# TensorE's order from modelled queues of VectorE, ScalarE, GpSimd and of PSUM's banks

## The chip, the cores and the metric

The kernel runs on one core of a Trainium2 chip. What counts is the device time of one execution in microseconds (us), as the median of several runs; smaller is better.

## The reference

One layer of a hybrid backbone for 256 context tokens and 2048 latent tokens of width 1024. One input projection feeds three token mixers; each is gated, and one output projection closes the layer.

```python
h = rmsnorm(x, g_pre) * (1 + scale) + shift
u_m, u_rs, u_rz, u_l = split(h @ w_in)
y_m = mlstm_branch(u_m)        # 6 heads of 64, chunkwise, one pass in each direction
y_r = rwkv_branch(u_rs, u_rz)  # 6 heads of 64, state S = S*w - (S kh) b + v kt, in each direction
y_l = rglru_branch(u_l)        # 256 channels: convolution, then a scan in each direction
o = concatenate([y_m, y_r, y_l]) @ w_out
return x + gate * rmsnorm(o, g_post), new states
```

Context tokens start from empty states and latent tokens from the cached ones; a direction's latent scan starts where its context scan ended.

## The kernel before

Everything is held with features or tokens on 128 partitions, and a projection of full precision is split into high and low parts, so that one block of 512 tokens costs three matmuls for each of eight slices of the contraction (`hhi`, `hlo` against `whi`, `wlo`, `w`). The stages, in the order of time:

- **build_h** normalises a block of tokens (`x`), transposes it (`tp`) and writes `hhi` and `hlo`. A block here is 256 context tokens or 512 latent tokens; blocks 1 and 0 come first, then 2, 3 and 4, each normed as its turn begins.
- **the projector** makes the columns of the input projection (`pp_v`, `pp_mk`, `pp_rz`, ...). Its matmuls depend on nothing late, so they are the filler of all stages up to the chains.
- **shift_post** makes the shifted RWKV inputs, and writes transposed values (`vs`) through SP's queue to the chunk store `ch`.
- **derive** runs 54 blocks of the RWKV preparation. For a block TensorE computes `pw`, ScalarE and VectorE make `KB` of it (the last step on line 972), and TensorE multiplies parts of it (`pt`). A round of 32 chunks (the trace has seven rounds) then goes to GpSimd, which solves a triangular system `W` in 30 pairs of instructions (lines 1058 and 1060), and comes back through a transposed `XT` into `pY` and `pX`.
- **mlstm** computes the chunks of the matrix memory: `pd` for its states, `pm` and `pn` for its outputs; GpSimd norms the result `H` (line 1344), and TensorE transposes it (`hT`).
- **chains**: three chains (two heads each) walk through 36 chunks forward and then 36 backward. A step loads `cg` from `ch`, makes a small product `cq`, ScalarE copies it into `q` (line 1630), a second product goes back into `cg` (VectorE, line 1644, in the first direction; ScalarE, line 1642, in the second), a third gives the next state (VectorE, line 1659). `ga` and `gb` prepare two steps at a time. The scans of the RG-LRU and the gates run beside the first direction, and the output projection of the mLSTM part (`po`) fills it.
- **out_last**: where all twelve parts of 128 tokens are in `yr`, they are normed, transposed (`yT`), gated into `zhi` and `zlo`, and multiplied by `w_out` (`pz`).

Tile, the framework, orders the instructions of all engines but TensorE. TensorE's order is planned by the class `Flow`, while the program is written out: each stage is a generator, and `run` always continues the ready one of the best rank (chains 1, workers such as derive and mlstm 2, out_last 3, filler 9). `F.now` is a clock that counts only the modelled time of the matmuls issued so far. Where a generator needs another engine's result, it yields a constant number of nanoseconds: what it assumes that the result takes. `LAT` (11000) stands between `pw` and `pt`, 40500 before `XT`, 7000 and 3000 around `pY`, 9000 before `hT`, `WAIT` or, until the scans are over, `LONG` between the parts of a chain's step, 4200 and 3800 (`L1`, `L2`) before `yT` and `pz`. No constant knows what else stands in an engine's queue, and a full PSUM does not move the clock.

## Time and profile before

| what | us |
| --- | --- |
| median of 3 runs (2066.2 to 2070.28) | 2069.45 |
| the profiled execution, its own time | 2059.59 |
| its span | 2057.9 |
| TensorE busy | 1801.6 |
| VectorE, ScalarE, GpSimd busy | 1367.0, 977.6, 795.0 |
| TensorE's mean granted clock | 0.933 |

The execution is cut into eight stretches where the work changes: at 103 us the start-up is over; at 577 the last `pp_v` ends, at 638 derive's first `pw` runs, at 1042 its last `pX`; at 1378 the chains' first `ga` runs, at 1726 they turn round, at 2018 the last `cq` is over. In each stretch the length less TensorE's busy time is its idle time; the eight idle times add up to 256.4 us. A wait row says which engine waited at which line for which result, and how long in total, how often, and at most. The last row's kind, the chain that ended last, gives the time per matmul when matmuls follow one another: a row of six 512-wide ones or of sixteen small ones.

### The profile page before, as it was taken

What the parts mean: (1) busy time and instruction counts of PE and PEld (TensorE: products, weight loads), DVE (VectorE), ACT (ScalarE), POOL (GpSimd) and SP (SyncE); (2) the same over time, 40 slices, a digit from 0 to 9 for tenths busy, and PEclk for the clock granted to TensorE, in tenths of its full rate; (3) what the DMA queues carried; (4) which work ended last, traced back from release to release, by engine and by line L of the source; (5) the groups of instructions that cost most, each with busy time, mean ns of one, the idle gap of its engine ahead of it and who ended that gap; (6) DMA issues with size and microseconds to landing.
All of it is one profiled execution on the core that took longest, in us unless ns stands there. A gap on an engine that the chain in (4) does not pass through costs nothing. (4 is left out here: it accounts for less than half of the span.)

```text
span 2057.9 us, 46221 instructions
## 1 busy us (share of the span) xinstructions
PE 1801.6 (88%) x16648; PEld 1201.0 (58%) x16778; DVE 1367.0 (66%) x3271; ACT 977.6 (48%) x2634; POOL 795.0 (39%) x1200
## 2 busy tenths in 40 slices
PE   5899999999999878788899798878778788999996
PEld 3555655656666556555566565555555556777774
DVE  3747366777643898998324766647885576777774
ACT  5732446565434667776242545542332233444442
POOL 0210011112110688888722444342653232444442
PEclk9899999999999988889999899989888999999997
DMA  7343344564548778887254666645986545576662
GB/s 284 118 142 90 126 123 133 153 168 148 132 127 247 215 207 223 225 214 176 80 154 135 188 171 170 171 118 154 292 268 193 164 136 149 163 196 203 197 190 72
DMA packets 353370, 350.60 MB, mean 170 GB/s; under 512 B 109554, under 2 KB 294978, under 8 KB 350728
## 3 DMA queue, kind: packets, MB, share of 16 engines
q1 hardware_dynamic: 353142, 347.65, 59.2%
q8 instruction: 133, 2.18, 0.5%
q14 instruction: 95, 0.78, 0.1%
HBM read 211.18 MB, written 136.37 MB: 169 GB/s over the span
## 5 line engine op out<-in xcount | busy, mean ns | idle before, releaser
L1635 POOL TENSOR_SCALAR sd<-cg,Dall 128x128 f32<-128x128 f32 x210 | 135.8, 654 | 267.1 <-DVE cg L1659 164.0
L1659 DVE SCALAR_TENSOR_TENSOR cg<-cq,Dall,sd 64x64 f32<-64x64 f32 x408 | 114.5, 281 | 46.4 <-PE cq L168 36.6
L1060 POOL TENSOR_TENSOR W<-W,tmp 128x30 f32<-128x30 f32 (+14 forms) x210 | 139.0, 662 | 16.1
L1058 POOL TENSOR_TENSOR tmp<-W 128x30 f32<-128x30 f32 (+14 forms) x210 | 133.0, 633 | 15.9
L168 PE MATMUL cq<-cg,bt 128*64 128x64 f32 x840 | 68.5, 246 | 49.7 <-DVE cg L1644 44.6
L1283 ACT ACTIVATE nb<-nb,aT 128x128 f32<-128x128 f32 x216 | 71.6, 393 | 82.5 <-DMA nb<-nm_d 72.4
L168 PE MATMUL cq<-cg 128*64 128x64 f32 x1728 | 92.9, 230 | 8.2 <-DVE cg L1659 8.2
L168 PEld LDWEIGHTS cq<-cg,bt 128*64 128x64 f32 x840 | 44.1, 142 | 84.9 <-DVE cg L1644 54.8
L168 PE MATMUL ga<-cg 64*64 64x128 f32 (+1 forms) x864 | 76.9, 270 | 16.9 <-DMA cg<-ch 16.9
L1630 ACT ACTIVATE q<-cq 128x64 f32<-128x64 f32 x216 | 45.5, 223 | 95.7 <-PE cq L168 92.3
L1592 DVE TENSOR_TENSOR cg<-gb,rmask 64x256 f32<-64x256 f32 x108 | 44.7, 413 | 66.3 <-PE gb L168 61.1
L168 PEld LDWEIGHTS cq<-cg 128*64 128x64 f32 x1728 | 72.9, 141 | 24.3 <-issue 9.5
L168 PE MATMUL pz<-owhi,zhi 128*128 128x512 f32 x180 | 82.1, 456 | 4.5 <-ACT zhi L1822 4.5
L1598 ACT ACTIVATE bt<-ga 128x256 f32<-128x256 f32 x108 | 41.3, 383 | 87.0 <-DVE G L1595 83.4
L168 PE MATMUL pt<-KB 64*64 64x64 f32 x864 | 41.9, 244 | 45.7 <-DVE KB L972 45.6
L1284 POOL TENSOR_SCALAR_AFFINE_SELECT nb<-nb 128x256 f32<-128x256 f32 x108 | 44.8, 421 | 93.0 <-ACT nb L1283 63.6
L168 PE MATMUL gb<-cg 64*64 64x128 f32 (+1 forms) x864 | 75.7, 270 | 0.9 <-DMA cg<-ch 0.9
L168 PE MATMUL pz<-owhi,zlo 128*128 128x512 f32 x180 | 73.5, 409 | 3.3 <-DVE zlo L1823 3.3
L168 PE MATMUL pz<-owlo,zhi 128*128 128x512 f32 x180 | 72.9, 405 | 0.0
L168 PEld LDWEIGHTS ga<-cg 64*64 64x64 f32 x864 | 48.2, 142 | 41.9 <-issue 27.9
L168 PE MATMUL cq<-q,cg 128*64 128x64 f32 x864 | 59.4, 236 | 9.9 <-ACT q L1630 9.9
L168 PE MATMUL pp_v<-hhi,whi_v 128*128 128x512 f32 (+1 forms) x120 | 67.4, 562 | 0.3 <-ACT whi_v L514 0.3
(511 smaller groups left out, 6180.0 us busy)
## 6 DMA issues: line engine op xcount, KB each, us to landing
cg<-ch SPq DMA_DIRECT2D x216, 192.0 KB
wa<-wa SPq DMA_DIRECT2D x54, 256.0 KB
z<-z SPq DMA_DIRECT2D x27, 512.0 KB
ch<-KB SPq DMA_DIRECT2D x108, 128.0 KB
ch<-KB SPq DMA_DIRECT2D x54, 256.0 KB
nb<-nm_d SPq DMA_DIRECT2D x108, 128.0 KB
lr<-L SPq DMA_DIRECT2D x16, 768.0 KB
lL<-lr SPq DMA_DIRECT2D x16, 768.0 KB
```

The source lines that it names most:

```text
L168: self.nc.tensor.matmul(out, lhsT, rhs, start=start, stop=stop, **kw)
L1058: nc.gpsimd.tensor_tensor(out=tv, in0=W[:, j + 1:32, j:j + 1].to_broadcast([128, m, j]), in1=W[:, j:j + 1, 0:j].to_broadcast([128, m, j]), ...
L1060: nc.gpsimd.tensor_tensor(out=W[:, j + 1:32, 0:j], in0=W[:, j + 1:32, 0:j], in1=tv, op=ALU.add)
L1283: nc.scalar.activation(nb[:, d, j], nb[:, d, j], AF.Exp, bias=aT[:, c, d, 2 * p + j:2 * p + j + 1])
L1284: nc.gpsimd.affine_select(out=nb[:, d], in_=nb[:, d], pattern=[[0, 2], [1 - 2 * d, 128]], base=0, channel_multiplier=-1 + 2 * d, compare_o ...
L1592: nc.vector.tensor_tensor(out=cg[o, :, RK[h]], in0=src[o], in1=mask[o, d].rearrange("p a c -> p (a c)")[:, None].to_broadcast([64, 2, 128] ...
L1598: nc.scalar.activation(bt, ga[:, 1], AF.Copy)
L1630: nc.scalar.activation(q, qk, AF.Copy, scale=-1.0)
L1635: nc.gpsimd.tensor_scalar(sd, cg.rearrange("p (n c) -> p n c", c=64)[:, 0::9], Dk, None, op0=ALU.mult)
L1659: nc.vector.scalar_tensor_tensor(out=nxt[h][b], in0=ps[b], scalar=Dk[b], in1=sd[b, 1 - h], op0=ALU.mult, op1=ALU.add)
```

## The change

Every VectorE, ScalarE and GpSimd instruction now passes through a proxy that writes down when it would start and end: a modelled cost, a queue for each engine, behind its inputs. PSUM's eight buffers are followed in the same way. `when(tile)` tells how far a tile's modelled end lies ahead of `F.now`, and takes the place of nearly all constants; `least` keeps a lower bound. `stand`, called before each matmul, moves `F.now` to the time at which the matmul's inputs and its bank are there. `First` marks instructions that Tile gives priority, so that the model lets them overtake.

Apart from that, `norm(b + 1)` is issued in the middle of block b (`norm(2)` right after the first two blocks) and `fetch` one block earlier; `H` is split in two tiles and `yr` in eighteen. The gates' and the scans' own constants and the loading of `w_out` stay. Instructions are the same: 11,330 matmuls, 1448 DMAs, and as many VectorE, ScalarE and GpSimd operations; only their order and their waits differ.

```diff
+class Queue:
+        def call(*a, **k):
+            r = f(*a, **k)
...
+            self.F.issued(self.kind, name, out, [x for x in aps if x is not out], k.get("accum_out"))
+            return r
...
+class Banks:
+    def tile(self, *a, **k):
+        t = self.pool.tile(*a, **k)
+        self.names.append(t.tensor.name)
+        if len(self.names) > self.n:
+            self.F.before[t.tensor.name] = self.names[-1 - self.n]
+        return t
...
+    TO, BETWEEN, FROM = 260.0, 90.0, 130.0
+    def cost(self, kind, op, n):
+        if kind == "a":
+            return 190.0 + 0.78 * n
+        if kind == "g":
+            return 150.0 + 1.05 * n if op in ("memset", "affine_select") else 330.0 + 2.0 * n
...
+        return 155.0 + (0.65 if op in ("tensor_copy", "tensor_scalar", "memset") else 0.97) * n
+    def issued(self, kind, op, out, ins, extra):
...
+        if kind == "v" and all(x.space != PSUM for x in [out] + ins) and any(a < t + d and t < b for a, b in self.taken["g"]):
+            d *= 1.35
+        if self.first:
+            for a, b in q:
+                if a <= t < b:
+                    t = b
+                    break
+        else:
+            for a, b in q:
+                if t + d <= a:
+                    break
+                t = max(t, b)
...
+    def when(self, *tiles, least=0.0):
+        return max([least] + [self.wrote.get(x.tensor.name, 0.0) + self.FROM - self.now for x in tiles])
+    def stand(self, out, *ins):
+        b = self.before.pop(out.tensor.name, None)
+        t = max([self.wrote.get(x.tensor.name, 0.0) + self.FROM for x in ins] + [self.read.get(b, 0.0) + self.FROM])
+        self.now = max(self.now, t)
...
     def mm(self, out, lhsT, rhs, start=True, stop=True, **kw):
+        self.stand(out, lhsT, rhs)
...
+            elif k + 1 == NK:
+                fetch(3)
...
+        norm(2)
         for b in range(2, len(BLOCKS)):
-            norm(b)
-            if b + 1 < len(BLOCKS):
-                fetch(b + 1)
+            if b + 2 < len(BLOCKS):
+                fetch(b + 2)
+            yield F.when(*xs[b])
             for k in range(NK):
+                if k == 4 and b + 1 < len(BLOCKS):
+                    norm(b + 1)
...
-                yield 1500.0
+                yield F.when(vr, *nxt) if d else F.when(vr)
...
             sid, l0, nm, KB = block()
-            yield LAT
+            yield F.when(KB, least=3000.0)
...
-        yield 40500.0
+        yield F.when(W)
...
-        yield 9000.0
+        yield F.when(HH[g])
...
-            wait = LONG if X["lru"].t is None else WAIT
+            wait = WAIT
...
-            yield wait[0], 1
+            yield F.when(q, least=wait[0]), 1
...
-            yield wait[1], 1
+            yield F.when(cg, least=wait[1]), 1
...
-        yield L1, 1
+        yield max(0.0, F.last + F.FROM - F.now), 1
...
-        yield L2
+        yield F.when(*[x for p in parts for x in p[1:]])
```

What that does to TensorE's order is shown at three places; a name's numbers tell the block or step, and a row ends with the shape and the count. The first is derive's first round, before; `pt` and `pw` come in runs, with filler after the run:

```order
L168 MATMUL pt_0_2560_6048<-KB_0_2560_5827 64x64 x8
L168 MATMUL pw_0_5121_6065<-wa_0_5121_5751,w_2_01_5729 128x256 x4
L168 MATMUL pt_0_2561_6094<-KB_0_2561_5865 64x64 x8
L168 MATMUL pw_0_7680_6109<-wa_0_7680_5883,w_2_00_5689 128x256 x4
L168 MATMUL pt_0_5120_6132<-KB_0_5120_5909 64x64 x8
L168 MATMUL pw_0_7681_6147<-wa_0_7681_5885,w_2_01_5729 128x256 x4
L168 MATMUL pp_mk_2_6189<-hhi,whi_mk_5576 128x512
L168 MATMUL pp_mk_2_6189<-hhi,wlo_mk_5577 128x512
```

The same stretch of the program after the change:

```order
L289 MATMUL pt_0_7680_6058<-KB_0_7680_5924 64x64 x8
L289 MATMUL pw_0_10241_6073<-wa_0_10241_5888,w_2_01_5585 128x256 x4
L289 MATMUL pp_mq_2_6115<-hhi,whi_mq_5339 128x512
L289 MATMUL pp_mq_2_6115<-hhi,wlo_mq_5340 128x512
L289 LDWEIGHTS w_mq_5341
L289 MATMUL pp_mq_2_6115<-hlo,w_mq_5341 128x512
```

Now one `pt` and one `pw` stand together, and eight matmuls of filler follow before the next pair.

The second is step 25 of the three chains in their first direction. The digit behind `cq` is the chain, the number behind it the step; a row that reads `q` is a chain's second product, and one that reads `bt` follows VectorE's copy into `cg`. Before:

```order
L168 MATMUL po150_17931<-owhi2_15395,yhi15_17761 128x512
L168 MATMUL po150_17931<-owlo2_15396,yhi15_17761 128x512
L168 MATMUL po150_17931<-owhi2_15395,ylo15_17762 128x512
L168 MATMUL cq1_26_18001<-cg11_14710 64x64 x4
L168 MATMUL cq2_25_17977<-q2_25_17982,cg20_14711 64x64 x2
L168 MATMUL cq0_26_17959<-cg01_14708,bt0_26_17837 64x64 x2
L168 MATMUL cq0_26_17959<-cg01_14708,G4_14729 64x64 x2
L168 MATMUL cq2_25_17977<-cg20_14711,bt2_24_17721 64x64 x2
L168 MATMUL cq2_25_17977<-cg20_14711,G3_14728 64x64 x2
```

After:

```order
L289 MATMUL cq2_25_17778<-q2_25_17783,cg20_14566 64x64 x2
L289 MATMUL cq0_26_17787<-q0_26_17792,cg01_14563 64x64 x2
L289 MATMUL cq1_26_17813<-cg11_14565 64x64 x4
L289 MATMUL po110_17754<-owhi2_15975,yhi11_17647 128x512
L289 MATMUL po110_17754<-owlo2_15976,yhi11_17647 128x512
L289 MATMUL po110_17754<-owhi2_15975,ylo11_17648 128x512
L289 MATMUL cq2_25_17778<-cg20_14566,bt2_24_17523 64x64 x2
L289 MATMUL cq2_25_17778<-cg20_14566,G3_14583 64x64 x2
L289 MATMUL cq0_26_17787<-cg01_14563,bt0_26_17638 64x64 x2
```

Between chain 2's product with `q` and its product with `bt` four small matmuls stood; now there are six small ones and three 512-wide ones.

The third is the end of the chains and the last tiles of out_last, where `yT3` must become `zhi3` before `pz30`. Before:

```order
L168 MATMUL pz41_23390<-owhi7_17888,zlo4_23271 128x512
L168 MATMUL cq2_71_23424<-cg21_14712 64x64 x4
L168 MATMUL yT3_23431<-ident_62,yr_14696 64x64 x12
L168 MATMUL cq2_71_23424<-q2_71_23429,cg21_14712 64x64 x2
L168 MATMUL cq2_71_23424<-cg21_14712,G2_14727 64x64 x2
L168 MATMUL pz30_23460<-owhi3_17657,zhi3_23448 128x512
L168 MATMUL pz30_23460<-owlo3_17658,zhi3_23448 128x512
```

After:

```order
L289 MATMUL pz41_23432<-owhi7_18397,zlo4_23362 128x512
L289 MATMUL yT3_23469<-ident_62,yr3_14537 64x64 x12
L289 MATMUL yT2_23490<-ident_62,yr2_14536 64x64 x12
L289 MATMUL pz30_23512<-owhi3_18202,zhi3_23486 128x512
L289 MATMUL pz30_23512<-owlo3_18203,zhi3_23486 128x512
L289 MATMUL pz30_23512<-owhi3_18202,zlo3_23487 128x512
L289 MATMUL pz30_23512<-owhi4_18261,zhi3_23486 128x512
L289 MATMUL pz30_23512<-owlo4_18262,zhi3_23486 128x512
L289 MATMUL pz30_23512<-owhi4_18261,zlo3_23487 128x512
L289 MATMUL pz20_23520<-owhi3_18202,zhi2_23507 128x512
```

The last chain step, `cq2_71`, now stands ahead of the products of tile 4, so that the last two tiles, 3 and 2, are transposed together, and their products alternate in sixes.

## Rows read from the trace of the kernel before

**Rows 1.** The page, first part: engine, busy time, share of the span, instructions.

```profile
PE 1801.6 (88%) x16648; PEld 1201.0 (58%) x16778; DVE 1367.0 (66%) x3271; ACT 977.6 (48%) x2634; POOL 795.0 (39%) x1200
```

**Rows 2.** Windows by stage: stretch, its length, busy time by engine, granted TensorE clock, DMA.

```profile
0.00:103.00 103.00, 74.42 (x473) 46.99 (x479) 60.69 (x149) 63.80 (x112) 16.52 (x20) 0.93 0.56 201
103.00:577.00 474.00, 458.46 (x2100) 274.80 (x2131) 298.11 (x466) 232.53 (x396) 70.70 (x60) 0.98 0.47 136
577.00:638.00 61.00, 60.93 (x303) 38.52 (x308) 16.60 (x32) 16.85 (x32) 3.71 (x6) 1.00 0.58 149
638.00:1042.00 404.00, 336.21 (x3736) 230.16 (x3779) 315.98 (x446) 256.54 (x771) 297.76 (x448) 0.88 0.72 192
1042.00:1378.00 336.00, 294.91 (x2437) 194.20 (x2471) 190.73 (x716) 156.59 (x445) 137.81 (x334) 0.95 0.59 162
1378.00:1726.00 348.00, 276.58 (x3550) 195.30 (x3556) 243.38 (x728) 109.93 (x354) 132.06 (x177) 0.89 0.67 195
1726.00:2018.00 292.00, 277.52 (x3967) 204.66 (x3964) 224.11 (x708) 134.13 (x506) 127.92 (x151) 0.98 0.64 184
2018.00:2058.00 40.00, 22.58 (x110) 16.41 (x104) 17.41 (x29) 7.22 (x20) 8.53 (x6) 0.70 0.20 72
```

**Rows 3.** Waits of the first 103 us: engine, line, releaser: total us, times, longest.

```profile
PE tp L175 <- DVE x L401: 13.0, 9, 9.6
```

**Rows 4.** Timeline of SP's queue before derive: start, length, engine, line, operation, tiles.

```profile
586.25 0.61 SPq L827 DMA_DIRECT2D ch<-vs  x1
...
621.90 2.57 SPq L827 DMA_DIRECT2D ch<-vs  x4
...
627.51 2.04 SPq L886 DMA_DIRECT2D wa<-wa  x2
```

**Rows 5.** Waits of TensorE in derive.

```profile
PE pt L168 <- DVE KB L972: 45.6, 22, 5.7
...
PE pY L168 <- DVE XT L1031: 14.1, 3, 5.8
```

**Rows 6.** GpSimd's lines in derive: line, tiles, shapes, count; busy us, mean ns; idle before.

```profile
L1060 POOL TENSOR_TENSOR W<-W,tmp 128x30 f32<-128x30 f32 (+14 forms) x210 | 139.0, 662 | 16.1
...
L1050 POOL TENSOR_SCALAR_AFFINE_SELECT W<-W 128x1024 f32<-128x1024 f32 x7 | 9.4, 1343 | 62.5 <-DVE W L1049 62.5
```

**Rows 7.** The same of VectorE in derive, its costliest line.

```profile
L972 DVE TENSOR_TENSOR KB<-cs,KB 128x512 f32<-128x512 f32 x54 | 48.2, 898 | 3.2 <-ACT cs L958 3.2
```

**Rows 8.** GpSimd's lines from 986 to 1025, derive's last round of substitution.

```profile
L1060 POOL TENSOR_TENSOR W<-W,tmp 128x30 f32<-128x30 f32 (+14 forms) x30 | 15.7, 522 | 2.4
```

**Rows 9.** Waits of the mLSTM stage, one of TensorE.

```profile
PE hT L175 <- POOL H L1344: 11.9, 5, 3.4
```

**Rows 10.** Waits of TensorE in the chains' first direction.

```profile
PE cq L168 <- DVE cg L1644: 44.6, 43, 7.3
PE ga L168 <- DMA cg<-ch: 12.9, 7, 2.9
PE cq L168 <- ACT q L1630: 9.9, 6, 2.7
PE cq L168 <- DVE cg L1659: 3.9, 3, 2.1
```

**Rows 11.** Timeline of TensorE at the end; brackets hold the idle time before and its releaser.

```profile
2021.29 0.80 PE L168 MATMUL pz<-owhi,zhi 128*128 128x512 f32 x1 [1.68 <-ACT zhi L1822]
...
2024.76 0.80 PE L168 MATMUL pz<-owhi,zlo 128*128 128x512 f32 x1 [2.26 <-DVE zlo L1823]
...
2026.21 0.63 PE L168 MATMUL pz<-owhi,zlo 128*128 128x512 f32 x1
2026.64 0.63 PE L168 MATMUL pz<-owhi,zhi 128*128 128x512 f32 x1
```

**Rows 12.** Chain that ended last, from 1378: start, length, what (x: matmuls in a row).

```profile
1388.53 0.97 PE cq L168 x16
...
1663.26 1.40 PE po L168 x6
```

More of the change, by code (lines that the diff above doesn't have):

```diff
@@ L94, in __init__, with __getattr__, __enter__, __exit__ @@
         self.t = None
+class Queue:
+    def __init__(self, F, kind, engine):
+        self.F, self.kind, self.engine = F, kind, engine
+    def __getattr__(self, name):
+        f = getattr(self.engine, name)
+        def call(*a, **k):
+            r = f(*a, **k)
+            aps = [x for x in list(a) + list(k.values()) if isinstance(x, bass.AP)]
+            out = k.get("out", aps[0])
+            self.F.issued(self.kind, name, out, [x for x in aps if x is not out], k.get("accum_out"))
+            return r
+        return call
+class Engines:
+    def __init__(self, F, nc):
+        self.nc = nc
+        self.vector, self.scalar, self.gpsimd = Queue(F, "v", nc.vector), Queue(F, "a", nc.scalar), Queue(F, "g", nc.gpsimd)
+    def __getattr__(self, name):
+        return getattr(self.nc, name)
+class Banks:
+    def __init__(self, F, pool, n):
+        self.F, self.pool, self.n, self.names = F, pool, n, []
+    def tile(self, *a, **k):
[4 more added lines that the diff above has]
+        return t
+class First:
+    def __init__(self, X, offset):
+        self.F, self.c = X["F"], X["tc"].high_priority(offset=offset)
+    def __enter__(self):
+        self.F.first = True
+        return self.c.__enter__()
+    def __exit__(self, *e):
+        self.F.first = False
+        return self.c.__exit__(*e)
 class Slots:
@@ L129, in __init__ @@
         self.cur, self.pace, self.hold = 0, [0.0, 0.0, 0.0], False
+        self.taken = {k: [] for k in "vag"}
+        self.wrote, self.read, self.before, self.first, self.last = {}, {}, {}, False, 0.0
+    TO, BETWEEN, FROM = 260.0, 90.0, 130.0
[4 more added lines that the diff above has]
+            return 150.0 + 1.05 * n if op in ("memset", "affine_select") else 330.0 + 2.0 * n
+        if op == "transpose":
+            return 2.0 * n
+        if op == "tensor_tensor_scan":
+            return 120.0 + 2.3 * n
+        return 155.0 + (0.65 if op in ("tensor_copy", "tensor_scalar", "memset") else 0.97) * n
+    def issued(self, kind, op, out, ins, extra):
+        if not hasattr(out, "tensor"):
+            return
+        t = self.now
+        for x in ins:
+            t = max(t, self.wrote.get(x.tensor.name, 0.0) + self.BETWEEN)
+        o = out.tensor.name
+        d = self.cost(kind, op, max(self.free(x) for x in [out] + ins))
+        q = self.taken[kind]
+        while q and q[0][1] < self.now:
+            q.pop(0)
+        if kind == "v" and all(x.space != PSUM for x in [out] + ins) and any(a < t + d and t < b for a, b in self.taken["g"]):
[10 more added lines that the diff above has]
+                t = max(t, b)
+        q.append((t, t + d))
+        q.sort()
+        self.last = t + d
+        for x in [out, extra]:
+            if x is not None:
+                self.wrote[x.tensor.name] = max(self.wrote.get(x.tensor.name, 0.0), t + d)
+        for x in [out] + ins:
+            self.read[x.tensor.name] = max(self.read.get(x.tensor.name, 0.0), t + d)
+    def when(self, *tiles, least=0.0):
[4 more added lines that the diff above has]
+        self.now = max(self.now, t)
     def share(self, x, hold=False):
@@ L168, in mm @@
         self.nc.tensor.matmul(out, lhsT, rhs, start=start, stop=stop, **kw)
+        self.wrote[out.tensor.name] = self.now + self.TO - self.BETWEEN
     def tr(self, out, in_, ident):
+        self.stand(out, in_)
         if self.form != [128, 128]:
@@ L175, in tr @@
         self.nc.tensor.transpose(out, in_, ident)
+        self.wrote[out.tensor.name] = self.now + self.TO - self.BETWEEN
     def fire(self, ev, lat=0.0):
@@ L773, in shift_post @@
         nxt = square(0)
-        yield 5000.0
+        yield F.when(*nxt)
         for b, (t0, n) in enumerate(BLOCKS):
@@ L802, in shift_post @@
         nxt = leading(X, sh, rk[:, 0:TP], f"b{p}0")
-        yield 4000.0
+        yield F.when(*nxt)
         for b, (t0, n) in enumerate(BLOCKS):
@@ L900, in merge @@
         hs = [(slice(64 * h, 64 * h + 32), slice(64 * h + 32, 64 * h + 64)) for h in range(2)]
-        yield 7000.0
+        yield F.when(XT, o, least=1000.0)
         pY = X["ps"].tile([128, 16, 32], F32, tag="b", name=f"pY{sid}{g}")
@@ L1290, in output @@
         nxt = start(p, get, todo, vs)
-        yield 5000.0
+        yield F.when(nxt[2]) if nxt else 0.0
         while nxt:
@@ L1324, in output @@
                 F.spawn(norm(p, g), 0)
-            yield 2500.0
+            yield F.when(nxt[2], least=1500.0) if nxt else 0.0
         end[0] -= 1
@@ L1452, in lru_gates @@
             nc.sync.dma_start(X["LR"][c][:, d, :, t0:t0 + n], L)
-            yield LR2
+            yield F.when(L)
     F.fire(end)
@@ L1515, in chains @@
     CP, NS, NB, NP = TP // 64, T // 64, 2, 5
-    yr = X["yr"] = rc.tile([128, 3, NS, 64], F32, name="yr")
+    yr = X["yr"] = [rc.tile([128, 3, 2, 64], F32, name=f"yr{t}") for t in range(NT)]
     X["ready"] = [Event() for _ in range(NT)]
@@ L1602, in chain @@
         load(2)
-        yield 4000.0
+        yield F.when(of(0), least=4000.0)
         yield from prepare(0)
-        yield 2000.0, 1
+        yield F.when(of(0)), 1
         for i in range(2 * NS):
@@ L1674, in chain @@
                 load(i + 3)
-                yield wait[2], 1
+                yield F.when(of(i + 1), least=wait[2]), 1
             else:
-                yield wait[2] - 500.0
+                t = F.now + wait[2]
+                yield F.when(of(i + 2), least=wait[2] - 500.0)
                 yield from prepare(i + 2)
-                yield 500.0, 1
+                yield F.when(of(i + 1), least=t - F.now), 1
     for p in range(3):
```

62 lines of the change are left out of this document (33 added, 29 removed).

## The prediction

> **What bounds the kernel now.** I read the page's busy shares first: TensorE works 1801.6 us of the span, 88%, and no other engine more than 66% [rows 1]. The matmuls are the same after the change, so it can move only TensorE's idle time, and the clock where idle time has lowered it. The windows by stage say where that idle time lies (length less busy, from the first row to the last): 28.6, 15.5, 0.1, 67.8, 41.1, 71.4, 14.5 and 17.4 us, 256.4 in all [rows 2]. The stretch 577 to 638 is full, and so nearly is the chains' second direction; derive, the mLSTM stage and the chains' first direction hold 180 us of the 256. Then the waits: in derive TensorE stands 45.6 us at `pt` for `KB` and 14.1 at `pY` for `XT` [rows 5]; in the mLSTM stage 11.9 at `hT` [rows 9]; in the first direction 44.6, 9.9 and 3.9 us for VectorE and ScalarE results of the chains themselves, and 12.9 for DMAs [rows 10].
>
> A wait is worth something only where TensorE is what the stage hangs on. In derive it isn't, as I read it. GpSimd is busy 297.8 of 404 us [rows 2]; its idle time is mostly the 55 us before the first round (62.5 us before line 1050 in all, seven rounds) [rows 6]. After that it hardly stops, and seven rounds fill the stage. VectorE's 316.0 us [rows 2] over 54 blocks [rows 7] are 5.85 us a block.
>
> **How the order is priced.** Times per matmul come from runs of matmuls at full speed: 1.40 us for six 512-wide ones, 0.23 each (0.115 for 256-wide), and 0.97 for sixteen small ones, 0.06 each [rows 12]. Counting the two orders with these, TensorE's work from one landmark to the next becomes: start to last `pp_v`, 442.4 in both; last `pp_v` to first `pw`, 56.6 to 37.3; to last `pX`, 281.7 to 274.8; to first `ga`, 216.5 to 215.2; to the turn of the chains, 190.4 to 208.0; to the last `cq`, 218.4 to 214.5; from there to the end, 14.5 to 28.4. So 27.5 us of filler leave the first three of the stretches that change, 17.6 go into the chains' first direction, 13.9 behind the last `cq`. A stretch whose length is set elsewhere gains idle time by what is taken out of it, and loses idle time by what is put in.
>
> **The change part by part**, as change of idle time.
>
> *Start: -3.* TensorE waits 13.0 us for normed tokens, in nine waits, the longest 9.6 [rows 3]. That one belongs to the first blocks, which are not normed earlier; the other 3.4 go if blocks 2 to 4 are normed ahead. Bounds 0 and -3.4. The norms are ScalarE and VectorE work that the stage does anyway, and `fetch(3)` puts its loads on SP earlier, at a time when its queue holds only weights.
>
> *Entry to derive: +14.* The stretch from the last `pp_v` to the first `pw` loses 84 filler matmuls of 512, 19.3 us. It was full before. Its length is set by SP: the write-backs of `vs` run one behind the other from 586.25, the last group at 621.90 for 2.57 us, and the loads of `wa` that `pw` needs are issued at 627.51, behind them [rows 4]. The number of these DMAs is the same, so SP's 40 us stay, and the first `pw` cannot come much earlier; the removed filler leaves a hole. What shortens it is that the write-backs may begin earlier: the transposes before them now wait for the modelled end of `vs` instead of 1500 ns. Bounds 0 (all 19 us gained by an earlier start) and +19; I take 14, near the end that SP's row supports.
>
> *Derive: +8.* If GpSimd sets the length, 404 us stay, and the 6.9 us of filler that leave (at the stage's own speed, 336.2 busy for 281.7 counted, 8.2 us) become idle time. The waits at `pt` and `pY` may change place without a price. The first round can't begin earlier by much: eight blocks at 5.85 us are 47 us, and it began 44 after the first `pw`. Downward bound -5, a sixth of the first round's lead; upward +16, from the next paragraph.
>
> The last round of substitution has VectorE nearly to itself, and line 1060 takes 522 ns there [rows 8] against a mean of 662 over all rounds [rows 6]. If the new order puts VectorE work beside the last round too, its 30 pairs cost 60 times 0.14, 8.4 us more. The Trainium skill says in "SBUF — State Buffer", section "Who interferes with whom", that a VectorE instruction with two SBUF inputs contends with GpSimd instructions that read SBUF, and that the shared port pair is an exclusive lock; the two means here are what one would see by it. By that rule the stage would end 8 us later, by the row of the undisturbed round not at all.
>
> *mLSTM: -7.* 11.9 us of waits at `hT` [rows 9], where 9000 ns were assumed. The least work that stands between the norm's last input and `hT` grows from 0.9 to 2.6 us in the new order. That is less than the longest wait, 3.4 us, so I take a little over half. Bounds 0 and -14.
>
> *Chains, first direction: -23.* The queue waits are 44.6 + 9.9 + 3.9 = 58.4 us [rows 10]. The model knows the scans that stand in VectorE's queue, which `LONG` only guessed, and puts filler between a chain's product and the product that needs its copy, as the order of step 25 shows. If the stretch keeps its 348 us, the 17.6 us of work put in are 17.6 us of idle time filled; if half of the waits go, it is 29. I take the middle, 23. Bounds 0 (each wait only moves to the next product) and -58. The 12.9 us for `cg` from its DMA stay, as these loads are issued as before. VectorE is busy 243 of 348 us there [rows 2], so it does not set the length.
>
> *Tail: -2.* After the last `cq` TensorE stands 1.68 us for `zhi` and 2.26 for `zlo`, and the next matmuls then take 0.43 us apiece (2026.21 to 2026.64) [rows 11] instead of 0.23, at a granted clock of 0.70 in that stretch [rows 2]. In the new order `yT3` and `yT2` still stand right before `pz30`, so that wait stays, but two tiles alternate behind it and the chain's own last wait is out of it. Bounds -6 and +6, where both tiles' last norms follow the end.
>
> *Sum:* -3 + 14 + 8 - 7 - 23 - 2 = -13 us. The profiled execution took 2059.59 us with a span of 2057.9, which is 10 under the median, 2069.45; the difference belongs to the runs and not to the program, so I put the sum on the median: 2069.45 - 13 = 2056. A profiled execution would by this show about 2047.
>
> **The rivals.** (a) *The queue waits of the first direction vanish.* Then its term is -58 and the time 2056 - 35 = 2021. For it: all three are waits for engines that the model follows, and VectorE has 105 us free. Against it: the model's durations are formulas, and the longest of these waits is 7.3 us [rows 10], more than a step has filler for.
>
> (b) *The holes at the entry and in derive stay, and nothing is won behind them: slower.* Filler put between the chains' products delays the next chain by as much as it covers, because the three chains share TensorE and their steps hang on one another's place in the order. Then the mLSTM and chain terms are 0 and the time is 2056 + 30 = 2086. For it: one filler group of three is 0.7 us, and the waits at line 1644 average 1.0 us (44.6 in 43), so much of what is covered is hardly longer than the cover. Against it: the second direction has the same chains with more filler and stands only 14.5 us in 292 [rows 2]. It decides from the point at which less than 10 of the 30 us come.
>
> (c) *TensorE becomes what derive hangs on: slower.* Between a `pw` and its own `pt` there were 9.6 to 13.6 us of matmul work in every one of the 54 blocks; now 20 have less than 8, 6.0 on the mean, and others up to 23. If each of the 20 holds TensorE for what it lost against 9.6, that is 3.6 times 20, 72 us more. The stage's slack is 67.8 us of idle time plus the 8.2 us of filler gone, and 67.8 of it are already used by today's waits: 72 - 8 = 64 us over, against 8 in the sum, so 2056 + 56 = 2112. It outweighs the gains once the extra holds pass some 29 us. Against it: a hold for one block is cover for the next, since two are always under way, the long covers give back, and VectorE needs only 5.85 us a block.
>
> (d) *The model says what the constants said.* Terms cancel and the time stays at 2069.
>
> **How the numbers follow.** A measurement of this kernel can tell about 0.2% (4 us) from no change. Forecast 0.50 (of it 0.44 faster, 0.06 same); (a) 0.13, faster; (b) 0.17 (0.14 slower, 0.03 same); (c) 0.12 (0.10 slower, 0.01 each for the others); (d) 0.08 (0.04 same, 0.02 each side). Faster 0.60, same 0.14, slower 0.26. The range must reach (b) at 2086 and most of the way to (a) with the -14 of the mLSTM bound: 2010 to 2095, which leaves out most of (c) and the far end of (a). The forecast's own range, with half of each term's bounds, is 2035 to 2070.
>
> **What the profile after would show.** Right: a hole of 10 to 19 us between the last `pp_v` and the first `pw`; GpSimd's rounds in derive still back to back at about 51 us each, with the waits at `pt` no larger in effect; waits at line 1644 in the first direction down from 44.6 to about 25; idle time of TensorE in all about 243 us. Wrong: pauses on GpSimd between rounds (then (c)), a first direction as long as before plus what was put in (then (b)), or a first `pw` that comes 15 us or more after the last `pp_v` sooner than now with no hole (then the entry term falls away and the time is nearer 2042).

## The result: slower by 1.1%

The changed kernel takes 2087.12 us, the median of 11 runs, against 2063.83 for the kernel before in the same runs: 1.0107 of it, 95% interval 1.0088 to 1.0127. That is 23 us more where the prediction had 13 less. In the profile after, all VectorE, ScalarE and GpSimd instructions carry line 107 (the proxy), TensorE's matmuls line 289 and its transposes line 298. Its profiled execution took 2075.49 us, the fastest of the 11, and before's 2059.59, so the two traces lie 16 us apart, not 23.

First the page's busy line, then the windows at the same landmarks as [rows 2]; derive's first `pw` runs at 632.45 here (stretch, length, busy time of PE, PEld, DVE, ACT, POOL, clock, DMA share, GB/s):

```profile
PE 1796.8 (87%) x16778; PEld 1191.4 (57%) x16778; DVE 1378.1 (66%) x3271; ACT 984.3 (47%) x2634; POOL 810.2 (39%) x1200
```

```profile
0.00:103.00 103.00, 73.75 (x497) 46.95 (x497) 58.96 (x149) 64.42 (x114) 20.61 (x22) 0.97 0.57 210
103.00:581.00 478.00, 453.45 (x2111) 270.93 (x2109) 297.60 (x464) 232.79 (x392) 69.91 (x58) 0.98 0.45 133
581.00:632.00 51.00, 42.39 (x225) 27.60 (x224) 17.00 (x32) 15.76 (x30) 3.71 (x6) 0.96 0.54 126
632.00:1046.00 414.00, 329.18 (x3748) 220.78 (x3748) 313.25 (x440) 255.66 (x767) 291.42 (x448) 0.87 0.71 189
1046.00:1378.00 332.00, 291.69 (x2450) 193.50 (x2442) 198.14 (x721) 158.25 (x446) 138.54 (x330) 0.95 0.60 165
1378.00:1720.00 342.00, 292.39 (x3653) 201.37 (x3655) 242.34 (x735) 111.89 (x357) 138.28 (x182) 0.91 0.70 198
1720.00:2024.00 304.00, 279.44 (x3909) 203.99 (x3909) 224.92 (x688) 133.75 (x499) 131.36 (x147) 0.98 0.58 167
2024.00:2074.00 50.00, 34.53 (x200) 26.27 (x200) 25.88 (x44) 11.75 (x31) 16.38 (x10) 0.85 0.43 147
```

TensorE's idle time, length less busy, against [rows 2], in us:

| stretch | before | after | change | predicted |
| --- | --- | --- | --- | --- |
| first 103 us | 28.6 | 29.3 | +0.7 | -3 |
| to the last `pp_v` | 15.5 | 24.6 | +9.1 | 0 |
| to derive | 0.1 | 8.6 | +8.5 | +14 |
| derive | 67.8 | 84.8 | +17.0 | +8 |
| mLSTM | 41.1 | 40.3 | -0.8 | -7 |
| chains, first direction | 71.4 | 49.6 | -21.8 | -23 |
| chains, second direction | 14.5 | 24.6 | +10.1 | 0 |
| behind the last `cq` | 17.4 | 15.5 | -1.9 | -2 |
| sum | 256.4 | 277.3 | +20.9 | -13 |

The terms of the first direction and of the tail came within 1.2 us. The entry and derive together cost 25.5 us where 22 were forecast, but less at the entry and twice as much in derive, 1 us beyond the bound given for it. Two stretches that had no term lost 19 us, and two small gains didn't come. TensorE's waits name the results that it stood for; the groups are those to the last `pp_v`, around derive's first `pw` (the wait for `w` stands behind it, in derive), derive, first and second direction (engine, line, releaser: us in total, times, longest):

```profile
PE lpr L289 <- DVE lxc L107: 19.3, 5, 9.7
```

```profile
PE pw L289 <- DMA wa<-wa: 8.7, 1, 8.7
PE pw L289 <- DMA w<-w: 6.3, 1, 6.3
```

```profile
PE pt L289 <- DVE KB L107: 73.2, 18, 12.2
...
PE pY L289 <- DVE XT L107: 2.5, 1, 2.5
```

```profile
PE cq L289 <- DVE cg L107: 31.3, 27, 3.8
PE cq L289 <- ACT q L107: 6.6, 8, 2.9
```

```profile
PE cq L289 <- DVE cg L107: 14.1, 13, 3.6
PE pz L289 <- DVE zlo L107: 4.3, 5, 1.6
```

`lpr`, a product of the RG-LRU's gates, waited nowhere before. In the first direction the waits of `cq` for VectorE fell from 44.6 and 3.9 [rows 10] to 31.3; in the second they rose from 5.6 to 14.1, and `pz`, which had no wait there, got one. The second direction's in the trace of before:

```profile
PE cq L168 <- DVE cg L1659: 4.3, 11, 0.4
...
PE cq L168 <- DVE cg L1644: 1.3, 1, 1.3
```

### The profile page after: what moved, and what is told of

Read it like the earlier page. It is cut to its first block, busy times and chain, and to the rows that moved or that the text cites. A ratio compares the mean times of both kernels' runs of the same rounds, so it can differ in the third digit from the quotient of the medians.

```text
span 2073.8 us, 46459 instructions
## 1 busy us (share of the span) xinstructions
PE 1796.8 (87%) x16778; PEld 1191.4 (57%) x16778; DVE 1378.1 (66%) x3271; ACT 984.3 (47%) x2634; POOL 810.2 (39%) x1200
## 5 line engine op out<-in xcount | busy, mean ns | idle before, releaser
L107 POOL TENSOR_SCALAR sd<-cg,Dall 128x128 f32<-128x128 f32 x210 | 147.4, 703 | 293.6 <-DVE cg L107 246.2
L107 POOL TENSOR_TENSOR tmp<-W 128x30 f32<-128x30 f32 (+14 forms) x210 | 128.0, 609 | 15.9
L107 ACT ACTIVATE nb<-nb,aT 128x128 f32<-128x128 f32 x216 | 71.8, 395 | 79.0 <-DMA nb<-nm_d 70.8
L289 PE MATMUL pt<-KB 64*64 64x64 f32 x864 | 40.3, 237 | 73.9 <-DVE KB L107 73.2
L289 PE MATMUL cq<-cg,bt 128*64 128x64 f32 x840 | 67.8, 243 | 34.6 <-DVE cg L107 30.3
L289 PE MATMUL ga<-cg 64*64 64x128 f32 (+1 forms) x864 | 75.7, 268 | 12.4 <-DMA cg<-ch 6.4
L107 DVE TENSOR_TENSOR cg<-gb,rmask 64x256 f32<-64x256 f32 x108 | 44.6, 413 | 58.5 <-PE gb L289 49.3
L289 PEld LDWEIGHTS pt<-KB 64*64 64x64 f32 x864 | 33.0, 146 | 83.8 <-issue 75.8
L107 ACT ACTIVATE DG<-pt 32x128 f32<-32x128 f32 x216 | 57.7, 267 | 28.7 <-PE pt L289 26.4
L107 DVE TENSOR_TENSOR KB<-E,z 128x256 f32<-128x256 f32 x108 | 67.9, 669 | 2.7 <-ACT E L107 2.7
```

The source lines that it names most:

```text
L107: r = f(*a, **k)
L289: self.nc.tensor.matmul(out, lhsT, rhs, start=start, stop=stop, **kw)
```

## The experiments

"Against before" is the ratio of the runs to runs of the kernel before on the same chip, with its 95% interval; the changed kernel is at 1.0107. A kernel is the changed one with the edit shown, unless the text says otherwise. Constants are those of the kernel before. Each run has a short name, e1 to e14, before its result.

**The gates' waits.** The diff also replaces the two constants of the RG-LRU gates, `LR1` and `LR2`. The part on the change said that the scans' and gates' constants stay; that holds for the mLSTM gates and the scans (`lru`), not for these two, and the prediction has no term for them.

```diff
-        yield F.when(xf)
+        yield 10000.0
...
-            yield F.when(L)
+            yield 7500.0
```

> The changed kernel with the two waits of the RG-LRU gates as constants again (10000 and 7500 ns of matmul work instead of the modelled ends of xf and L). Theory A (the changed kernel puts the gates' products, lpr, too near to their input, because VectorE's real queue is longer than the modelled one): the 19.3 us of waits at lpr in the projector stretch fall below 5, the stretch from 103 us to the last pp_v loses about 9 us of idle time, and the time falls by about 9, from 2087 to 2078. Rival B (the wait is only there because filler was moved to where TensorE waits anyway): the wait at lpr goes, another takes its place in the same stretch, and the time stays within 4 us.

e1: 1.0016 (0.9998 to 1.0034): 0.9% less than the changed kernel, twice what theory A said. The wait at `lpr` was 0.2 us, and the stretch from 100 us to the last `pp_v` shrank from 481 to 468:

```profile
100.00:568.00 468.00, 460.65 (x2144) 276.35 (x2180) 299.45 (x472) 233.68 (x397) 72.39 (x60) 0.99 0.48 138
```

Why the model put `lpr` too early is seen around its longest wait, in the changed kernel: SP's queue, ScalarE and TensorE (start, length, engine, line, operation, in brackets the idle time before and its releaser).

```profile
295.38 11.42 SPq L1585 DMA_DIRECT2D lr<-L  x2
```

```profile
302.78 0.47 ACT L107 ACTIVATE L<-lpr,hv 128x256 f32<-128x256 f32 x1 [7.94 <-DMA lr<-L]
```

```profile
310.70 2.04 PE L289 MATMUL lpr<-lxc,lwa 128*128 128x512 f32 x2 [9.67 <-DVE lxc L107]
```

`L` has one buffer. ScalarE stood 7.94 us until a DMA had emptied it; behind that instruction, in the same queue, stood the first step of the next `lxc`, and TensorE stood 9.67 us for `lxc`. The DMA kept ScalarE waiting before the change too, in the stretch to the last `pp_v`:

```profile
ACT L L1444 <- DMA lr<-L: 21.4, 6, 9.4
```

There it cost TensorE nothing: the constants spread the `lpr` products over 296 us (213.1 to 508.8), the model put them into 177 (209.7 to 386.7). The model has three engines' queues and PSUM, and no DMA. So the next run told it of this one DMA, and left the waits to the model:

```diff
+            if F.lfree > F.now:
+                F.taken["a"] = sorted(F.taken["a"] + [(F.now, F.lfree)])
             nc.scalar.activation(rg, pr, AF.Tanh, scale=0.5, bias=hc(f"ba_{d}{c}"))
...
             nc.sync.dma_start(X["LR"][c][:, d, :, t0:t0 + n], L)
+            F.lfree = F.wrote[L.tensor.name] + 10000.0
             yield F.when(L)
```

> The changed kernel, its gates' waits still taken from the model, but the model is told of one DMA: ScalarE's next write into L may start only 10000 ns after L's last result, and what is queued behind it on ScalarE waits too. The gates' products then spread over 2285 rows of TensorE's order instead of 1785. Theory A (the changed kernel's waits at lpr come from ScalarE standing for the DMA that empties L, which the model doesn't hold): the waits at lpr fall from 19.3 us to below 6, and the time falls by as much as with the constants, some 15 to 20 us against the changed kernel, to within 0.4% of the kernel before. Rival B (they come from wrong durations of VectorE or ScalarE instructions): the waits stay above 12 us and the time within 5 us of the changed kernel.

e5: 0.9997 (0.9975 to 1.0019). The wait is nearly gone (the stretch to the last `pp_v`):

```profile
PE lpr L289 <- DVE lxc L107: 2.4, 1, 2.4
```

Theory A holds: with the engines' durations as they were, a hold for the missing DMA was enough. Its 10000 ns are a constant again, so the run doesn't show that a modelled length of that DMA would do; and holding `L` spreads the products again, as the constants do. (Two buffers for `L` would have been the plainer test; it wasn't run.)

**The hole at the entry.**

```diff
-    load(20000.0)
-    load(20000.0)
+    load(39300.0)
+    load(39300.0)
```

> The changed kernel with the first two loads of derive assumed to take 39300 ns of matmul work instead of 20000, which puts the 84 filler matmuls back ahead of the first pw (56.6 us of counted work between the last pp_v and the first pw, as before the change, instead of 37.3). Theory A (the hole at the entry is SP's queue, which the model doesn't hold, so the model lets derive begin before its data can be there): the 15 us of waits at pw for wa and w disappear, the first pw runs no later than now (about 632 to 636), and the time falls by 12 to 15, to about 2073. Rival B (derive is bound by GpSimd, and the filler that is put back is missing there): the hole closes, but the waits in derive grow by as much, and the time stays within 4 us of 2087.

e2: 1.0092 (1.0057 to 1.0128), not told apart from the changed kernel. The hole closed, in the stretch from the last `pp_v` to the first `pw`:

```profile
584.00:645.00 61.00, 60.56 (x298) 38.05 (x304) 16.49 (x32) 17.73 (x33) 3.71 (x6) 1.00 0.60 154
```

Idle time turned up behind it: from the first `pw` to the turn of the chains TensorE idles 188 us, against 175 in the changed kernel. The time and this speak for rival B. But the first `pw` ran at 644.8 instead of 632.5, where theory A had it no later than before: the filler that closed the hole also held derive back by 12 us. And the second direction, cut at its last `cq`, idles 9.7 us here against 25.9, in an order in which nine of the seventeen gaps between tiles are even (see below); so what the hole costs by itself stays unsettled. The cause was the one that was predicted: in the changed kernel SP wrote `vs` back until 624.04 and only then came to `wa`:

```profile
618.83 5.21 SPq L957 DMA_DIRECT2D ch<-vs  x8
...
627.26 1.14 SPq L1016 DMA_DIRECT2D wa<-wa  x2
```

But the hole, 15 us in its two waits, was not a loss of 15 that this edit gives back.

**Derive's waits.**

```diff
-            yield F.when(KB, least=3000.0)
+            yield 11000.0
...
-        yield F.when(W)
+        yield 40500.0
```

and 7000 and 3000 around `pY`.

> The changed kernel with derive's four waits as constants again (11000 before pt, 40500 before XT, 7000 and 3000 around pY). Theory A (the short covers at pt, 21 of 54 below 8 us, hold TensorE and cost about 10 us): the waits at pt fall from 73 us to about 45, derive's idle time from 78 to about 68, and the time by 8 to 10, to about 2078. Rival B (GpSimd sets derive's length, so the waits at pt cost nothing): pt's waits fall, but the stretch stays at 405 us within 3, and the time within 4 us of 2087.

e4: 1.0091 (1.0058 to 1.0124), again not told apart. The waits changed places: TensorE's in derive are now

```profile
PE pY L289 <- DVE XT L107: 50.8, 6, 12.9
PE pt L289 <- DVE KB L107: 20.0, 9, 5.0
```

70.8 us at both, where the changed kernel has 75.7. The time is as rival B said: where TensorE waits in this stage is free of charge. Rival B's reason, that GpSimd sets the length, is not borne out by the rows. The stretch did not stay: by the first `pw` and the last `pX` it is 404 us before, 414 in the changed kernel and 424 here, in a profiled execution that was the slowest of its four.

```profile
633.00:1057.00 424.00, 342.24 (x3733) 228.83 (x3785) 312.31 (x444) 257.31 (x773) 294.47 (x448) 0.85 0.70 187
```

And GpSimd's first round began 11 us earlier in the changed kernel than before, yet derive's last `pX` starts 4 us later (1045.9 against 1042.2). Between the rounds GpSimd waits longer for VectorE's `XT`. The start of its first round and these waits, before and then after:

```profile
682.12 1.35 POOL L1050 TENSOR_SCALAR_AFFINE_SELECT W<-W 128x1024 f32<-128x1024 f32 x1 [55.16 <-DVE W L1049]
POOL XT L1035 <- DVE XT L1034: 7.7, 3, 4.9
```

```profile
670.78 1.63 POOL L107 TENSOR_SCALAR_AFFINE_SELECT W<-W 128x1024 f32<-128x1024 f32 x1 [44.41 <-DVE W L107]
POOL XT L107 <- DVE XT L107: 19.3, 6, 8.2
```

What makes derive longer stays open. Rival (c), 56 us more, was not what happened, but one of its signs, pauses on GpSimd between the rounds, did come.

**The second direction.** First out_last's waits.

```diff
-        yield max(0.0, F.last + F.FROM - F.now), 1
+        yield 4200.0, 1
...
-        yield F.when(*[x for p in parts for x in p[1:]])
+        yield 3800.0
```

> The changed kernel with out_last's two waits as constants again (4200 before yT, 3800 before pz). Theory A (the 10 us that the chains' second direction loses come from out_last: its products now follow their inputs so closely, and two tiles so near one another, that VectorE's work for them stands ahead of the chains' state updates): TensorE's idle time in the second direction falls from 25 to about 15, the waits at pz for zlo (4.3 us) vanish there, and the time falls by about 8, to 2079. Rival B (they come from the mLSTM output work that was moved behind the turn, 45 matmuls): idle time there stays at 23 to 26, the time within 3 us of 2087.

e3: 1.0073 (1.0044 to 1.0102), and 21.4 us of idle time there, up to the last `cq`: between the two. The order showed what theory A had half: with the modelled waits the two workers of out_last fall into step. The work between one tile's `yT` and the next, which had been 13 us all through, is 1, 25, 3, 25, 4, 23, 4, 23, ... in the changed kernel, and 2, 26, 2, 26, ... for nine tiles with the constants. The traces show the same: the starts of `yT` lie 15 to 18 us apart before, and 1, 33, 5, 35, 12, 29, 6, 34, ... in the changed kernel. So the next run spaced them:

```diff
-    def worker():
+    def worker(lag):
         while todo or ahead:
...
             F.fire(X["last"])
+            if lag:
+                yield lag
+                lag = 0.0
+                continue
...
-    for _ in range(n[0]):
-        F.spawn(worker(), RANK)
+    for k in range(n[0]):
+        F.spawn(worker(12000.0 * k), RANK)
```

> The changed kernel with one thing more: the second of out_last's two workers begins 12000 ns of matmul work after the first, so that the tiles' transposes (yT) come 13 us of work apart instead of in pairs (1 and 25 us, 3 and 25, 4 and 23, ...), and 12 us of the work behind the last cq go ahead of it. Theory A (the second direction idles because the norms and gates of two tiles stand together in VectorE's queue, ahead of the chains' state updates): its idle time falls from 26 us to below 16, and the time by about 10 against the changed kernel. Rival B (the idle time comes with the mLSTM output work that reaches into the second direction, 39 matmuls in both): it stays above 22.

e9: 0.9959 (0.9937 to 0.9981): 1.5% less than the changed kernel, three times what was expected, and faster than before. The second direction and what follows it, in the changed kernel and here, both cut where the last `cq` is over (2028 and 2020), then TensorE's waits in the second direction here:

```profile
1720.00:2028.00 308.00, 282.10 (x3933) 205.63 (x3935) 227.46 (x693) 135.72 (x505) 132.11 (x148) 0.98 0.59 168
2028.00:2074.00 46.00, 31.87 (x182) 24.63 (x176) 23.33 (x39) 9.78 (x25) 15.63 (x9) 0.83 0.39 136
```

```profile
1717.00:2020.00 303.00, 289.19 (x4017) 212.91 (x4017) 224.58 (x706) 140.06 (x514) 136.42 (x151) 0.98 0.65 180
2020.00:2052.00 32.00, 19.32 (x92) 14.52 (x90) 14.87 (x25) 6.60 (x17) 7.53 (x5) 0.79 0.32 113
```

```profile
PE cq L289 <- DVE cg L107: 1.8, 3, 0.9
...
PE pz L289 <- DVE zlo L107: 0.5, 2, 0.3
```

`cq`'s wait for VectorE fell from 14.1 to 1.8 and `pz`'s for `zlo` from 4.3 to 0.5; idle time there from 25.9 to 13.8 us, with as much mLSTM output work in it as before the edit, so rival B falls. The stretch behind the last `cq` fell from 46 to 32 us, nearly all of it work that now stands ahead. In VectorE's queue of the changed kernel one sees two tiles' steps ahead of a state update (third row; start, length, engine, line, operation):

```profile
1873.45 1.28 DVE L107 SCALAR_TENSOR_TENSOR zo<-zo,zss,GG 128x1024 f32<-128x1024 f32 x1
1874.65 0.68 DVE L107 TENSOR_TENSOR zo<-pz,zo 128x512 f32<-128x512 f32 x1
1875.25 0.59 DVE L107 SCALAR_TENSOR_TENSOR cg<-cq,Dall,sd 64x64 f32<-64x64 f32 x2
```

**The chains' model.** The changed kernel with `LONG` and `WAIT` again:

```diff
-            wait = WAIT
+            wait = LONG if X["lru"].t is None else WAIT
...
-            yield F.when(q, least=wait[0]), 1
+            yield wait[0], 1
...
-            yield F.when(cg, least=wait[1]), 1
+            yield wait[1], 1
```

> The changed kernel with the chains' waits as constants again (LONG until the scans are over, then WAIT). Theory A (the model of the queues is what the first direction gained by): TensorE's idle time in the first direction goes from 49 back to 65 or more, the waits of cq for VectorE's copy from 31 back to about 45, and the time rises by 10 or more, to about 2097. Rival B (the first direction gained because 17.6 us of filler arrived there, whatever the waits): its idle time stays at 49 to 56 and the time within 5 us of the changed kernel's.

e6: 1.0063 (1.0040 to 1.0087): the idle time of the first direction did rise, to 62 us, if not to the 65 of theory A, and the waits of `cq` for VectorE to 38.6:

```profile
1379.00:1724.00 345.00, 282.81 (x3634) 197.28 (x3649) 242.11 (x732) 111.05 (x356) 132.27 (x181) 0.92 0.68 195
```

So some 13 of the 21.8 us that the first direction gained go with the chains' model; the other 9 stay without it. And yet the time fell by 0.4%. The second direction idled 19 us instead of 26, with its tiles in pairs for seven gaps only; that would account for half of what the first lost, and what gave the rest isn't shown. Next, the model in the chains alone: constants in the other stages (build_h and the first product of `po` keep the model), and without the line that lets the clock stand; the matmuls' line is 288 there.

```diff
-        self.now = max(self.now, t)
```

> The changed kernel with constants in all stages but the chains, and without the clock's standing (stand no longer moves F.now). TensorE's order up to the chains is that of the kernel before by the counts (56.6, 281.7 and 216.5 us of work in the three stretches ahead of them). Theory A (the chains' model alone does not pay): against the kernel with only the norms ahead it stays within 0.2%. Rival B (it pays where nothing else is changed): the first direction's idle time falls by 10 us or more, and the time by 0.5%. Derive's idle time should be back at 68 us; if it is still near 84, then it isn't the order that costs derive its 17 us.

e12: 1.0038 (1.0022 to 1.0055). Rival B in the first direction, whose idle time fell to 56 us, and a loss of the same size in the second, at a wait that wasn't there before:

```profile
PE pz L288 <- DVE zlo L107: 17.2, 14, 1.3
PE pz L288 <- ACT zhi L107: 7.0, 14, 0.6
```

Derive is back at 66 us of idle time, so its extra 17 us did come with the order. `pz` came about 1.2 us too early in each of 14 tiles: 3800 fitted the old order. With 5000 in its place:

```diff
-        yield 3800.0
+        yield 5000.0
```

> The kernel with the chains' model alone, with 5000 instead of 3800 ns between the transposes of out_last and pz. Without that it lost 17.2 us in 14 waits of pz for zlo and 7.0 in 14 for zhi, in the second direction, while the first had gained 14 us. Theory A (the old constant fitted the old order, and the chains' model is worth its 14 us once pz comes later): these waits fall below 8 us in all, the second direction idles below 18 us, and the time is 0.4% or more below the kernel before. Rival B (whatever fills the first direction is missing in the second): the second direction's idle time stays above 25 us, or the time within 0.2% of the kernel before.

e14: 0.9934 (0.9921 to 0.9947); `pz` waits 0.2 us in the second direction. The two directions:

```profile
1391.00:1722.00 331.00, 271.86 (x3551) 192.60 (x3559) 239.92 (x732) 111.06 (x356) 129.57 (x176) 0.90 0.73 204
1722.00:2019.00 297.00, 281.77 (x3985) 207.55 (x3983) 226.09 (x709) 136.66 (x508) 133.45 (x152) 0.99 0.65 184
```

The first idles 59 us, 12 less than before, and the second 15 where it idled 31.4 without the edit: the 24.2 us at `pz` were one constant's, and 16 of them came back as idle time saved. Theory A: the chains' model with that constant (and the norms ahead, which by e10 give nothing, and the split of `H` and `yr`) is worth 14 us. What 5000 would do in the kernel before was not tried; `pz` waits for nothing there.

**Together.** Constants in the gates, the later loads, and constants in out_last:

> The changed kernel with the three repairs that gave something together: constants in the gates, the first loads of derive taken as 39300 ns away, constants in out_last. If the losses are separate, their sum against the changed kernel is 19 + 3 + 7 us, and the time is some 5 to 8 us below the kernel before, about 2055. If they share one loss (TensorE merely waits elsewhere), it stays at the best single one, within 0.2% of the kernel before.

e8: 0.9967 (0.9948 to 0.9986). That is what separate losses would give: 29 us less than the changed kernel, the sum of 19, 3 and 7. The 3 and the 7 are hardly clear of noise by themselves. The same with constants in the chains:

> The kernel with the three repairs (constants in the gates and in out_last, derive's first loads 39300 ns away) and the chains' waits as constants too. Theory A (the chains' model is worth nothing even where nothing spoils it, since what the first direction saves is work that the second then lacks as cover): within 0.2% of the kernel with the three repairs, 0.9967 of before. Rival B (it is worth the 12 to 22 us that the first direction's idle time fell by): 0.5% or more slower than that kernel, so slower than the kernel before.

e11: 1.0005 (0.9988 to 1.0022): 0.4% more, between the theories; the chains' model pays here, some 8 us, less than the 12 to 22 of rival B. All constants but the chains', with the clock standing:

> The changed kernel with constants again in the gates, in shift_post, in derive, in mLSTM and in out_last, so that the queues' model decides the chains alone (the norms a block ahead stay, and the model's clock still waits). Theory A (the chains' model is worth some 20 us, and all losses come from the other places): the entry has no hole, lpr no waits, the first direction idles about 50 us, and the time is 10 to 20 us below the kernel before, near 2045. Rival B (filler that is saved in one stage is missing in the next, so the sum stays): within 5 us of the kernel before.

e7: 0.9984 (0.9964 to 1.0005), rival B. The first direction idled 63 us, and the mLSTM stage 62.5 instead of 40.3; as I read it, a constant that was fitted to a clock of matmul work alone means less time on a clock that also counts waits, but no run shows that by itself. The norms alone, on the kernel before:

> The kernel before with the norms and fetches of token blocks 2 to 4 a block ahead, and nothing else of the change. Theory A (the norms ahead are worth the 3 us that the prediction gave them): the start loses 2 to 4 us of idle time, and the time is 0.1 to 0.2% below the kernel before. Rival B (in the repaired kernels the start is 9 to 14 us shorter than before, and this comes from the norms): the last pp_v ends 8 us or more earlier and the time is 0.4% lower.

e10: 1.0000 (0.9986 to 1.0014): no gain. The start's wait for normed tokens stays at 13.1 us; the 3.4 us that were to go did not.

Last, the two repairs that each did most, the gates' constants and the spaced workers:

> The changed kernel with the two repairs that each brought it back to the kernel before or below: constants in the gates, and out_last's second worker 12000 ns of work behind the first. Its order has the counts of the kernel with the spacing alone. Theory A (the two losses lie in different stretches and add up): 0.009 below the kernel with the spacing alone (0.9959 of before), so about 0.987 of before, near 2036; lpr's waits below 1 us and the second direction's idle time below 16 us. Rival B (the time that is won at the start is lost again before the chains end, since something with a fixed time of its own, such as the scans or a DMA, sets their end): 0.993 to 0.998, as either repair alone.

e13: 0.9878 (0.9861 to 0.9896), 2036.78 us: theory A to a tenth of a per cent, and the fastest kernel of this study, 1.2% below the one before. It differs from e1, at 1.0016, by the spacing alone, so the spacing gives 1.4% here again. Its page's busy line and three of its windows (to the last `pp_v`; derive; second direction):

```profile
PE 1788.2 (88%) x16631; PEld 1189.5 (59%) x16778; DVE 1368.3 (67%) x3271; ACT 983.3 (48%) x2634; POOL 807.0 (40%) x1200
```

```profile
100.00:561.00 461.00, 455.32 (x2112) 273.77 (x2144) 295.47 (x465) 230.99 (x392) 70.72 (x59) 0.99 0.48 140
612.00:1025.00 413.00, 327.11 (x3701) 220.56 (x3750) 313.75 (x440) 255.03 (x768) 293.04 (x448) 0.87 0.72 190
1699.00:1998.00 299.00, 289.42 (x4013) 212.69 (x4010) 223.86 (x704) 140.07 (x513) 136.10 (x151) 0.98 0.67 182
```

The stretch to the last `pp_v` idles 5.7 us, the second direction 9.6. Derive still idles 86 us; what that costs was not found.

## Why the prediction was wrong, step by step

- *What bounds the kernel*: right in that TensorE's idle time is what moved. That derive hangs on GpSimd is not shown: its waits move from `pt` to `pY` and back without a price (e4), but derive grew from 404 to 414 us, though GpSimd began 11 us earlier.
- *Entry, +14*: 8.5 us up to the first `pw` and 6.3 in the wait just behind it, from SP's queue as described. As a price it is not confirmed: closing the hole moved the time by 3 us and the first `pw` by 12 (e2).
- *Derive, +8*: came with 17.0, beyond its bound of 16. Rival (c) gave 64 us for covers that were too short; 75.7 us of waits stand there against 59.7 before [rows 5], and undoing the order there changed nothing in the time that can be measured.
- *First direction, -23*: came with -21.8, in part by luck. The model gave some 13 of it (e6), 12 where it stood alone (e14). Work put in rose by 16 us and VectorE's waits fell from 48.5 to 31.3, as forecast; but in the changed kernel this gain was worth nothing that can be seen, since the time fell when the chains' model was taken out (e6).
- *Start, -3, and mLSTM, -7*: +0.7 and -0.8. The norms ahead alone do nothing (e10), and TensorE's wait at `hT` stayed, 12.4 us against 11.9 [rows 9].
- *What failed*: two stretches that the sum put at nothing, to the last `pp_v` and the second direction. The gates' `LR1` and `LR2` were read as unchanged; the model that took their place knows no DMA, and cost 0.9% (e1, e5). And the second direction was passed over as nearly full, though the prediction's own count took 3.9 us of work out of it; out_last's waits were priced only behind the last `cq`, at -2, though the part on the change had shown that two tiles alternate there. The same pairing runs through the whole second direction, where VectorE then works for two tiles at once while the chains' state updates queue; undoing it gave 1.5% (e9). Both undone give 1.2% less than before (e13), which is the sign that was forecast, and more than its 13 us.
- *Rival (b)* forecast 2086, and 2087 came, by luck; its mechanism is not what happened. It let the first direction gain nothing; that stretch gained 21.8 us. Only its thought that such a gain need not show in the time has some support (e6).

What stays open: why the spacing alone gave 30 us by the medians, when the profiled executions of the two kernels, 22 us apart, show 12.1 us of idle time less in the second direction and 1.4 behind it, and the rest in stretches that the edit doesn't touch (the changed kernel's profiled execution was its fastest). What lengthened derive, and what that costs. And whether the split of `H` and `yr` does anything by itself was not tried.

## What to carry to other kernels

A model that replaces tuned constants must hold every resource that ends a wait: in the chains, with one constant behind them fitted anew, it was worth 14 us here, and where it lacked one DMA it cost 19. Price each replaced constant on its own, also those that look like the others, and ask of two workers that share an engine whether the new waits let them fall into step. Idle time of the engine that works most is not lost time as such: closing a hole of 15 us here moved the time by 3; the filler that closed it held the next stage back by 12, and idle time turned up later.

## What the runs showed of the hardware

TensorE's busy time for the same matmuls was 1795.2 us at a mean granted clock of 0.937 in the profiled execution with spaced tiles (e9) and 1811.0 at 0.926 in the one with the chains' model alone (e12): 16 us, beside what they idle. How much of that is the order's isn't shown, as the clock differs between executions of one kernel too: 0.931 to 0.943 in the ten of e9, 0.924 to 0.933 in the twelve of e12, 0.927 to 0.938 in the eleven of the changed kernel. The last round of GpSimd's substitution stayed undisturbed (VectorE is busy 11.5 of its 43 us), so the 8 us that VectorE's work beside it might have cost did not come: the last round's window of the changed kernel (line, tiles, shapes, count; busy, mean ns; idle before) has 525 ns for the instruction of [rows 8], which had 522.

```profile
L107 POOL TENSOR_TENSOR W<-W,tmp 128x30 f32<-128x30 f32 (+14 forms) x31 | 16.3, 525 | 2.4
```
